# Issuing the first store of a streaming softmax without waiting for the third load

## The chip, the cores and the metric

The kernel runs on one core of a Trainium2 chip. The metric is the device time of one execution in microseconds. It was 317.92 us before the change, the median of 3 runs (317.4 to 318.28).

## The reference

```python
x = np.random.randn(32, 512, 1024).astype(np.float32)      # temperature = 0.5

def reference(x, temperature):
    scaled = x / temperature
    shifted = scaled - np.max(scaled, axis=-1, keepdims=True)
    exp_x = np.exp(shifted)
    return (exp_x / np.sum(exp_x, axis=-1, keepdims=True)).astype(np.float32)
```

It is a softmax over rows of 1024 numbers, 16384 rows, 67.1 MB in and 67.1 MB out.

## The kernel before

The 16384 rows are cut into eleven passes. A pass puts `k` rows side by side into each of the 128 partitions: 11 in the first pass, 12 in the nine after it, 9 in the last. A pass is one load into one tile `xt` (SP, L62), work in place, and one store of the same tile (L110). The stores of passes 0 to 5 are issued by Pool (`BY_POOL = 6`), the others by ACT. There are four tiles, `BUFS = 4`: four loads are issued at the start, and load i+4 goes out (from `store`) once store i has landed and its tile is free.

A pass is worked in groups of rows: 4, 4, 3 in the first, 6, 6 in the middle ones, 4, 3, 2 in the last (`PASSES`). For a group, `maximum` takes the row maxima on DVE (L71) and scales them to a bias (L74); `exponential` does one activation for each row on ACT, which also sums (L80); `divide` takes the reciprocal (L92) and multiplies on DVE, row by row (L98) or, in passes 2, 3, 4 and 6, the whole group at once (L95). The order is written out by hand (`tc.manual_schedule`): up to the last pass, the divide of a group comes after the maximum and the exponentials of the next group, and with the divide of a pass's last group comes its store. So the first store is due after the maximum of pass 1's first group and the divide of pass 0's third group.

The first store alone has an operation of Pool ahead of it: a copy of one column of `tiles[2]`, the tile of the third load, into a small tile `seen` that nothing reads (L108). The copy waits until the third load has landed; the store's issue is behind it in Pool's order.

Of the kernel before, what the change touches and what calls it, by code (L numbers as in the profile page):

```python
# [1 line left out]

# [4 lines left out]

PASSES = [[4, 4, 3]] + [[6, 6]] * 9 + [[4, 3, 2]]  # L10
BUFS = 4

WHOLE = (2, 3, 4, 6)


BY_POOL = 6

ALONE = 9

HELD = len(PASSES) - 1  # L20


@with_exitstack
def kernel(
    ctx: ExitStack,
    tc: tile.TileContext,
    x: bass.AP,
    temperature: bass.AP,
    out: bass.AP,
):  # L30
    nc = tc.nc
    f32 = mybir.dt.float32
    scale = 1.0 / float(temperature)
    extreme = mybir.AluOpType.max if scale > 0 else mybir.AluOpType.min

    P = 128
    xf = x.flatten_outer_dims()
    of = out.flatten_outer_dims()
    n, d = xf.shape
    rows = [sum(ks) for ks in PASSES]  # L40
    assert sum(rows) * P == n

    data = ctx.enter_context(tc.tile_pool(name="data", bufs=BUFS))
    stats = ctx.enter_context(tc.tile_pool(name="stats", bufs=4))


    groups = []
    for i, ks in enumerate(PASSES):
        for j, k in enumerate(ks):
            groups.append((i, sum(ks[:j]), k))  # L50

    def dram(t, i):
        block = t[P * sum(rows[:i]) : P * sum(rows[: i + 1]), :]
        return block.rearrange("(p k) d -> p k d", p=P, k=rows[i])

    tiles, small = [], []

    def load():
        i = len(tiles)
        if i < len(PASSES):  # L60
            xt = data.tile([P, rows[i], d], f32, name="xt")
            nc.sync.dma_start(out=xt, in_=dram(xf, i))  # L62
            tiles.append(xt)

    def maximum(g):
        i, a, k = groups[g]
        top, bias, sums, recip = (
            stats.tile([P, k], f32, name=name) for name in ("top", "bias", "sums", "recip")
        )
        small.append((bias, sums, recip))  # L70
        nc.vector.tensor_reduce(  # L71
            out=top, in_=tiles[i][:, a : a + k, :], axis=mybir.AxisListType.X, op=extreme
        )
        nc.vector.tensor_scalar_mul(bias, in0=top, scalar1=-scale)  # L74

    def exponential(g):
        i, a, k = groups[g]
        bias, sums, _ = small[g]
        for b in range(k):
            nc.scalar.activation(  # L80
                tiles[i][:, a + b, :],
                tiles[i][:, a + b, :],
                mybir.ActivationFunctionType.Exp,
                bias=bias[:, b : b + 1],
                scale=scale,
                accum_out=sums[:, b : b + 1],
            )

    def divide(g):
        i, a, k = groups[g]  # L90
        _, sums, recip = small[g]
        nc.vector.reciprocal(recip, sums)  # L92
        if i in WHOLE:
            xt = tiles[i][:, a : a + k, :]
            nc.vector.tensor_mul(xt, xt, recip.unsqueeze(2).to_broadcast([P, k, d]))  # L95
            return
        for b in range(k):
            nc.vector.tensor_scalar_mul(  # L98
                tiles[i][:, a + b, :], in0=tiles[i][:, a + b, :], scalar1=recip[:, b : b + 1]
            )  # L100

    def store(g):
        i, a, k = groups[g]
        if a + k == rows[i]:
            if i == 0:


                nc.gpsimd.tensor_copy(stats.tile([P, 1], f32, name="seen"), tiles[2][:, 0, 0:1])  # L108
            queue = nc.gpsimd if i < BY_POOL else nc.scalar
            queue.dma_start(out=dram(of, i), in_=tiles[i])  # L110
            load()

    with tc.manual_schedule():
        for _ in range(BUFS):
            load()
        waiting = []

        def finish():  # L120
            for g in waiting:
                divide(g)
                store(g)
            waiting.clear()

        for g, (i, a, k) in enumerate(groups):
            if i >= ALONE and a == 0:
                finish()
            maximum(g)
            exponential(g)  # L130
            if i < HELD:
                finish()
            waiting.append(g)
        finish()


# [1 line left out]
_INS = ['x', 'temperature']  # L138
_OUTS = [((32, 512, 1024), 'float32')]

_NUMBERS = {'temperature': 0.5}


# [26 lines left out]
```

## Time and profile before

| | us |
|---|---|
| median of 3 runs | 317.92 (317.4 to 318.28) |
| the profiled execution, its own time | 318.96 |
| its span in the profile | 317.2 |
| DVE busy | 252.3 (80%) |
| ACT busy | 148.3 (47%) |
| Pool busy | 3.7 (1%) |
| moved by DMA | 134.24 MB, 423 GB/s on the mean |

The span runs from the first to the last instruction of the program; the execution's own time also has what lies around it. The profile cuts the span into 40 slices of 7.93 us; a digit is a busy share in tenths. DVE is the vector engine, ACT the scalar engine, Pool the GpSimd engine, and SP the one that issues the loads. The 16 DMA engines of the core carry the packets of all queues; each load or store is split over all 16, and the trace holds start, duration, queue and size of every packet, and when each of the 16 parts of a transfer landed.

### The profile page before, as it was taken

The numbers are of one execution on the slowest core, as the hardware profiler recorded it, in microseconds if no ns is written. First come the engines' busy times: TensorE is split into PE (matmuls) and PEld (weight loads), VectorE is DVE, ScalarE is ACT, GpSimd is POOL, SyncE is SP. The second block draws the span as 40 slices with busy tenths as digits, with TensorE's granted clock in tenths as the row PEclk, the third lists the DMA queues.
The fourth block names the chain that finished last, engine by engine and source line by source line (L and its number), as shares of the span: only waits on it lengthen the run. The fifth ranks groups of instructions, "written<-read, shape, count | busy, mean of one in ns | idle before, by whom it ended". The sixth has DMA issues, their size and how long they took to land. (4 is left out here: it accounts for less than half of the span.)

```text
span 317.2 us, 542 instructions
## 1 busy us (share of the span) xinstructions
DVE 252.3 (80%) x160; ACT 148.3 (47%) x257; POOL 3.7 (1%) x11
## 2 busy tenths in 40 slices
DVE  0099999999999799969949994997199689779900
ACT  0048477468174353807171770438035805916600
POOL 0000010000000000000000000000000000000000
DMA  9999999999999999999999999999999999999994
GB/s 364 401 459 397 459 434 377 417 439 438 440 403 465 428 409 471 410 440 440 403 471 415 415 477 397 446 441 409 465 421 409 471 418 431 442 414 459 421 432 181
DMA packets 3171, 134.24 MB, mean 423 GB/s; under 512 B 352, under 2 KB 352, under 8 KB 352
## 3 DMA queue, kind: packets, MB, share of 16 engines
q1 hardware_dynamic: 1584, 67.11, 49.5%
q0 software_dynamic: 864, 37.22, 27.1%
q10 hardware_dynamic: 720, 29.88, 21.8%
q14 instruction: 3, 0.02, 0.0%
HBM read 67.11 MB, written 67.11 MB: 423 GB/s over the span
## 5 line engine op out<-in xcount | busy, mean ns | idle before, releaser
L80 ACT ACTIVATE xt<-xt,bias 128x1024 f32<-128x1024 f32 x128 | 145.2, 1135 | 133.7 <-DVE bias L74 64.6
L71 DVE TENSOR_REDUCE top<-xt 128x6 f32<-128x6144 f32 (+3 forms) x24 | 140.1, 5837 | 40.7 <-DMA xt<-in_x_dram 40.7
L98 DVE TENSOR_SCALAR xt<-xt,recip 128x1024 f32<-128x1024 f32 x80 | 54.5, 748 | 0.6
L95 DVE TENSOR_TENSOR xt<-xt,recip 128x6144 f32<-128x6144 f32 x8 | 52.5, 6559 | 0.6 <-DVE recip L92 0.2
L80 ACT ACTIVATION_READ_ACCUMULATOR xt<-xt,bias 128x1 f32 x128 | 23.8, 186 | 0.0
L80 ACT ACT_TABLE_LOAD x1 | 1.3, 1283 | 16.7 <-DMA xt<-in_x_dram 16.7
L92 DVE RECIPROCAL recip<-sums 128x6 f32<-128x6 f32 (+3 forms) x24 | 4.3, 180 | 5.8 <-ACT xt L80 5.8
L110 POOL DMA_DIRECT2D out_dram<-xt x6 | 3.3, 554 | 129.0 <-ACT xt L80 83.8
L74 DVE TENSOR_SCALAR bias<-top 128x6 f32<-128x6 f32 (+3 forms) x24 | 4.1, 171 | 0.8
L108 POOL COPY seen<-xt 128x1 f32<-128x1 f32 x1 | 0.2, 183 | 45.3 <-DMA xt<-in_x_dram 45.3
L151 POOL MEMSET const-bfloat16-1.0<- 128x1 bf16 x1 | 0.1, 102 | 0.0
L151 POOL MEMSET const-uint8-127<- 128x1 uint8 x1 | 0.1, 102 | 0.0
L151 POOL MEMSET const-float32-0.0<- 128x1 f32 x1 | 0.1, 99 | 0.2 <-issue 0.2
L151 POOL MEMSET const-float32-1.0<- 128x1 f32 x1 | 0.1, 99 | 0.0
## 6 DMA issues: line engine op xcount, KB each, us to landing
xt<-in_x_dram SPq DMA_DIRECT2D x9, 6144.0 KB, 37.1
out_dram<-xt POOLq DMA_DIRECT2D x5, 6144.0 KB, 36.7
out_dram<-xt ACTq DMA_DIRECT2D x4, 6144.0 KB, 32.6
xt<-in_x_dram SPq DMA_DIRECT2D x1, 5632.0 KB, 15.8
out_dram<-xt POOLq DMA_DIRECT2D x1, 5632.0 KB, 28.5
xt<-in_x_dram SPq DMA_DIRECT2D x1, 4608.0 KB, 39.5
out_dram<-xt ACTq DMA_DIRECT2D x1, 4608.0 KB, 15.5
```

The source lines that it names most:

```text
L71: nc.vector.tensor_reduce(out=top, in_=tiles[i][:, a : a + k, :], axis=mybir.AxisListType.X, op=extreme)
L74: nc.vector.tensor_scalar_mul(bias, in0=top, scalar1=-scale)
L80: nc.scalar.activation(tiles[i][:, a + b, :], tiles[i][:, a + b, :], mybir.ActivationFunctionType.Exp, bias=bias[:, b : b + 1], scale=scal ...
L92: nc.vector.reciprocal(recip, sums)
L95: nc.vector.tensor_mul(xt, xt, recip.unsqueeze(2).to_broadcast([P, k, d]))
L98: nc.vector.tensor_scalar_mul(tiles[i][:, a + b, :], in0=tiles[i][:, a + b, :], scalar1=recip[:, b : b + 1])
L108: nc.gpsimd.tensor_copy(stats.tile([P, 1], f32, name="seen"), tiles[2][:, 0, 0:1])
L110: queue.dma_start(out=dram(of, i), in_=tiles[i])
L151: nc = _bacc.Bacc("TRN2", target_bir_lowering=False, num_devices=1)
```

## The change

Pool's copy of the column of the third tile is taken out. Pool's first instruction after the start is now the issue of the first store, which waits for the divide of pass 0's last group. Nothing else in the order of any engine differs. The third store, also on Pool, now carries its own wait for the third load, which the copy had before.

```diff
     def store(g):
         i, a, k = groups[g]
         if a + k == rows[i]:
-            if i == 0:
-
-
-                nc.gpsimd.tensor_copy(stats.tile([P, 1], f32, name="seen"), tiles[2][:, 0, 0:1])
             queue = nc.gpsimd if i < BY_POOL else nc.scalar
             queue.dma_start(out=dram(of, i), in_=tiles[i])
             load()
```

## The prediction

> **What bounds the kernel now.** I read the strip of slices first, because a streaming kernel is bounded either by its transfers or by an engine that feeds them.
>
> ```profile
> DVE  0099999999999799969949994997199689779900
> ACT  0048477468174353807171770438035805916600
> ...
> DMA  9999999999999999999999999999999999999994
> GB/s 364 401 459 397 459 434 377 417 439 438 440 403 465 428 409 471 410 440 440 403 471 415 415 477 397 446 441 409 465 421 409 471 418 431 442 414 459 421 432 181
> ```
>
> The DMA row is at 9 in every slice but the last, so the transfers are the bound. The GB/s row scatters because a transfer's packet counts where it starts. Summed packet by packet over 10 us, the trace's packet records give 430 to 434 GB/s in every stretch from 10 us to 310 us, except 40 to 50 us (413) and 50 to 60 us (404). Those two stretches hold the only visible loss, and the edit lies in them. So I read that place in order of time next (columns: start, duration, engine and line, operation, idle time before it).
>
> ```profile
> 41.99 2.08 DVE L98 TENSOR_SCALAR xt<-xt,recip 128x1024 f32<-128x1024 f32 x3
> ...
> 43.98 6.54 DVE L71 TENSOR_REDUCE top<-xt 128x6 f32<-128x6144 f32 x1
> ...
> 45.70 0.18 POOL L108 COPY seen<-xt 128x1 f32<-128x1 f32 x1 [45.25 <-DMA xt<-in_x_dram]
> 46.28 0.67 POOL L110 DMA_DIRECT2D out_dram<-xt  x1 [0.40 <-issue]
> ...
> 66.09 0.53 POOL L110 DMA_DIRECT2D out_dram<-xt  x1 [19.15 <-DVE xt L98]
> ```
>
> The first tile is divided at 41.99 + 2.08 = 44.07. Pool copies at 45.70, when the third load has landed, and issues the first store at 46.28. The next store leaves 0.30 us after its divide (61.72 + 4.07 = 65.79, issued at 66.09). Then the waits (columns: total us, times, longest).
>
> ```profile
> POOL seen L108 <- DMA xt<-in_x_dram: 45.3, 1, 45.3
> ...
> DVE top L71 <- DMA xt<-in_x_dram: 40.7, 8, 16.6
> ```
>
> and SP's own:
>
> ```profile
> SPq L62 <- DMA out_dram<-xt: 238.8, 7, 72.2
> ```
>
> SP's line shows the ring that carries the kernel: SP holds load i+4 until store i has landed. DVE's line shows that DVE starves for loads, not the reverse. Last, the chain of waits at its end (start, duration, what):
>
> ```profile
> 208.96 35.04 DMA out_dram<-xt
> ...
> 244.14 39.52 DMA xt<-in_x_dram
> ...
> 283.68 4.43 DVE top L71
> ...
> 299.31 0.75 DVE xt L98
> ```
>
> A store lands, the last load is issued, lands at 283.66, and DVE and ACT finish by 300.7; the last store is issued at 300.76 and lands at 316.29.
>
> The whole time adds up from the transfers. A 48 KB packet of one DMA engine takes 1.812 us undisturbed (16 x 49152 B / 1.812 us = 434 GB/s). 134.22 MB / 434 GB/s = 309.3 us. Engines start at 1.95 us on the mean, the first packets take 0.74 us extra, and the disturbance near 50 us takes 1.13 us (the excess over 1.812 us of all packets that begin between 46 and 53 us is 18.0 us, over 16 engines). That is 313.1; the engines end their last packets at 312.9 to 313.9, with one at about 314.4 and the last one at 315.96. That one lag of some 2.6 us sets the end. The span is 317.2, the execution's own time 318.96, 1.0 above the median of 317.92 of the runs shown (317.4 to 318.28). I work in differences and put them on 317.92.
>
> **The change part by part.**
>
> *Removed: the copy on Pool.* 0.18 us of an engine that is busy 3.7 us in all, the wait for the third load, and 0.40 us between copy and issue. None is on the path by itself. Pool needs no new wait for the first store; the third store now itself waits for the third load, but it leaves at 93.12 and that load landed at 45.65: nothing.
>
> *Moved: the first store's issue.* 44.07 + 0.30 (row of the second store) = 44.37 in place of 46.28: 1.9 us earlier. One DMA moves, of 5632 KB; no other issue moves on Pool, and SP's four first loads are already queued (issued 0.74 to 2.1 us), so it passes nothing in a queue. What it moves past is the bytes of the fourth load.
>
> *When its bytes flow.* Its first packets began at 51.19, 4.9 us after the issue; with the same delay at 49.3. In the 4.9 us the engines were not idle: load packets ran until 48.3 at full rate. So the early store doesn't fill a hole; it swaps its bytes with bytes of the fourth load.
>
> *The fourth load.* From 51.2 on, load and store packets alternate. One store packet more ahead of its end (45056 B, 1.66 us) moves its landing from 71.29 to about 73.0. DVE first reads that tile at 79.13, so 6.1 us of cover remain; if that cover were gone, each us beyond it would be a us of DVE, which the later starvation by loads (40.7 us in all) would absorb again.
>
> *The store's landing, and the ring.* This is the decisive step. The store lands when the four loads and it are through: 2 x 5.767 + 3 x 6.291 = 30.41 MB / 434 GB/s = 70.1; + 1.95 + 0.74 + 1.13 = 73.9. Measured: 73.97 on the first engine, 74.80 on the last. As long as the fourth load is through before the store (71.3 before, 73.0 after), the order of the two has no effect on this instant. The fifth load is therefore issued at 74.87 as now, and from there on every transfer, wait and divide stands as before. Gain from the move itself: 0.
>
> A rule that speaks against the change: the Trainium skill, DMA: Bandwidth & Descriptors, section "Queues, rings and completion order", says that a DMA engine takes turns between the queues at packet granularity, so an early store takes every second packet from a load. The alternating packets agree. By the rule alone the fourth load would lose up to half of its rate for 1.9 us, about 1 us, also inside the cover.
>
> *The disturbance near 50 us.* In before, load packets that began at 48.3 to 50.6, 2 to 4 us after the issue, took 0.4 to 1.55 us longer than 1.812 us. None of the later stores shows this: around 66 to 72, 93 to 99 and 209 to 215 the rate is 424 GB/s or more. Whatever it is, it belongs to the first store, which the changed kernel has too, so I take 1.13 us again, about 1.9 us earlier. Its bounds: 0 (the later stores' rows), a gain of 1.1 us; and two slow packets on each engine in place of one at the worst row (2 x 1.55 = 3.1), a loss of 2.0 us. I take the nearest row, the same store's own: 0.
>
> A second rule bears here: the Trainium skill, SBUF — State Buffer, in its note on VectorE blocking DMA, says that descriptors of a Pool DMA cannot be written while VectorE runs an operation in a mode that uses both ports. In the trace VectorE runs one reduction from 43.98 to 50.52, over the old issue and the new one, and no other operation until 50.56; by the page's section on that contention a reduction doesn't block. By this rule the cost is 0 too; had the store been issued among the three divides it would have been up to 2.1 us.
>
> *The end.* The last load could come later only by the ring. The last store is issued at 300.76, its data could flow about 1.0 us later (the first load: 0.74 to 1.76), and the engine that ends last is free for it only at 305.07: 3.3 us of cover on that engine.
>
> Sum: 0 + 0 + 0 + 0 = 0, 317.9 us.
>
> **The rivals.**
>
> *Faster: the early start counts.* If the disturbance is the price of the store meeting a particular packet of the fourth load, or of the Pool work just ahead, it may go: 1.1 us, 316.8. If also the last engine's lag shrinks by part of its 2.6 us, 315.8. For it: the stretch 44 to 52 us is the only one that loses rate. Against it: loads ran at 434 GB/s until 48.3, so an earlier start by itself fills nothing.
>
> *Slower: the disturbance grows.* Place: the load packets in flight 2 to 4 us after the first store's issue. Now the third load's last packets and their completions (44.6 to 45.65) lie just there, and Pool's issue no longer comes after them. If each engine takes two slow packets instead of one, the cost is another 1.1 us at the mean and up to 2.0 us: 319.0 to 319.9. The trace already has a few engines with two slow packets in succession (1.0 + 0.4 us). It decides from a mean excess of 2.1 us on, or if the one late engine is hit by as much alone, since that engine sets the end. Against it: the third load is through at 45.65, before the expected new place (46.4).
>
> *The change does nothing to the order:* the copy could only be replaced by a wait of the same length if the divide were late; its end at 44.07 says it isn't. This rival gives 317.9 as well and differs only in the issue time.
>
> **How the numbers follow.** 0.3%, or 0.95 us, is about what a measurement of this kernel can tell from no change. No change, by the sum, including the last rival: 0.42, its own range 317.0 to 318.9. Slower by the disturbance or by the late engine: 0.34, since the excess of a single packet scatters from 0.4 to 1.55 us and the end hangs on one engine of sixteen, which can lose more easily than win. Faster: 0.24. Range 316.6 to 320.0: it takes in the price of a vanished disturbance (316.8) and of a doubled one at its worst (319.9); about 1 in 10 is left out on either side.
>
> **What would show it.** Right: Pool's first store issued at 44.3 to 44.5; the fourth load landing at about 73 and still before DVE's reduction at 79; the fifth load issued at 74.5 to 75.2; the same dip of rate, now around 46 to 51 us; the last store issued at 300 to 301.5. Wrong: the fifth load issued more than 1 us away from 74.87, a dip of rate that is absent or twice as deep, DVE waiting for the fourth tile, or one DMA engine that ends 4 us or more behind the others.

## The result and the profile after

The changed kernel is slower, by 0.7%: 320.69 us, the median of 22 runs (317.75 to 323.9), against 317.27 us for 22 runs of the kernel before (316.85 to 318.28). The ratio is 1.0072, 95% interval 1.005 to 1.0094; it leaves out the runs more than 1.5% above the fastest of the same kernel, and over all runs the medians stand 1.1% apart. The runs tell more than the median: the quickest (317.75) come near those of the kernel before, but 17 of 22 lie above 318.5 us, and none of the kernel before's 22. In later sittings the kernel before had such long executions too, 23 of 115, from 1 of 25 in one sitting to 9 of 31 in another, so every run below stands beside the kernel before of its own sitting. The profiled execution of the changed kernel is one of the short ones, 317.76 us with a span of 316.0 us. It cannot show the loss by itself; longer executions do, below.

The strip of the changed kernel:

```profile
DVE  0089999999999599969967994999299699689800
...
DMA  9899998999999999999999999999999999999995
GB/s 354 383 492 398 436 460 376 461 400 477 404 398 442 454 398 473 423 399 485 411 398 485 411 423 467 404 443 442 411 467 423 404 443 425 434 465 417 429 431 247
```

The transfers are still the bound. In order of time (start, duration, engine and line, operation, idle time before it), Pool's first instruction is now the store:

```profile
41.99 2.08 DVE L98 TENSOR_SCALAR xt<-xt,recip 128x1024 f32<-128x1024 f32 x3
...
43.99 6.55 DVE L71 TENSOR_REDUCE top<-xt 128x6 f32<-128x6144 f32 x1
...
44.38 0.67 POOL L106 DMA_DIRECT2D out_dram<-xt  x1 [43.94 <-DVE xt L98]
```

The waits (total us, times, longest) on loads and on landed stores have hardly moved:

```profile
DVE top L71 <- DMA xt<-in_x_dram: 39.4, 8, 16.6
```

```profile
SPq L62 <- DMA out_dram<-xt: 239.2, 7, 72.1
```

The end of the chain of waits in this short execution (start, duration, what):

```profile
210.05 34.35 DMA out_dram<-xt
...
244.53 37.57 DMA xt<-in_x_dram
...
282.12 4.43 DVE top L71
```

and in another execution of the same kernel that took 320.47 us (run again1):

```profile
209.66 34.91 DMA out_dram<-xt
...
244.70 40.48 DMA xt<-in_x_dram
...
285.21 4.43 DVE top L71
```

The last load is issued at the same time, but lands at 282.10 in one and at 285.19 in the other. A transfer has landed when the last of its 16 parts has. In the long execution the median part of that load landed at 277.36, the last but one at 280.10 and the last at 285.19: one DMA engine is 7.8 us behind the median. What that does to the rest shows in the windows near the end of the long execution (columns: window and length, busy time of DVE, ACT and Pool, clock, DMA share, GB/s):

```profile
300.00:302.00 2.00, 1.96 (x5) 0.21 (x2) 0.00 (x0) 1.00 0.91 393
302.00:304.00 2.00, 0.26 (x1) 0.00 (x0) 0.00 (x0) 1.00 0.70 301
304.00:308.00 4.00, 0.00 (x0) 0.00 (x0) 0.00 (x0) 1.00 1.04 445
```

At 302 to 304 us the DMA engines run dry: by the packet records 14 of 16 wait 0.4 to 1.1 us for the last store, which could only be issued at 302.29. Its last part landed at 317.82, in the short execution at 315.10. In the kernel before the same window reads

```profile
302.00:304.00 2.00, 0.00 (x0) 0.00 (x0) 0.00 (x0) 1.00 1.21 522
```

I call the landing of a transfer's last part minus that of its median part the lag. The table has it for the second store (landing near 100 us), the fifth (near 188 us) and the sixth (217 to 223 us), and then the landing of the end. "Excess" is the time by which load packets of 48 KB near the first store's start exceed 1.812 us: the sum over 16 engines divided by 16, and the largest single packet. All are single executions, us.

| run | first store issued | excess, mean / largest | lag, 2nd store | lag, 5th store | lag, 6th store | last part of last store | own time |
|---|---|---|---|---|---|---|---|
| before | 46.28 | 1.09 / 1.55 | 0.67 | 1.45 | 3.56 | 316.29 | 318.96 |
| delay | 45.99 | 1.23 / 1.49 | 0.54 | 0.53 | 0.93 | 314.78 | 317.45 |
| before_pool | 46.44 | 1.07 / 1.09 | 0.44 | 0.71 | 0.88 | 314.89 | 317.92 |
| delay12 | 48.44 | 1.15 / 1.30 | 0.38 | 0.59 | 0.83 | 314.47 | 317.13 |
| delay9 | 47.31 | 1.19 / 1.32 | 0.82 | 0.81 | 3.36 | 316.53 | 319.19 |
| delay3 | 45.08 | 1.17 / 1.27 | 0.81 | 1.26 | 3.97 | 316.96 | 319.63 |
| changed kernel | 44.38 | 0.41 / 0.89 | 1.95 | 1.95 | 1.96 | 315.10 | 317.76 |
| again2 | 44.63 | 0.70 / 1.30 | 2.09 | 2.07 | 4.09 | 316.40 | 319.06 |
| again1 | 44.66 | 1.04 / 1.50 | 0.94 | 2.07 | 4.61 | 317.82 | 320.47 |
| copy_tile1 | 44.24 | 0.74 / 1.06 | 0.61 | 2.58 | 5.92 | 318.03 | 320.70 |
| after_pool | 44.59 | 0.50 / 1.14 | 2.17 | 3.22 | 3.78 | 318.80 | 321.83 |

The time is the landing of the last part plus 2.7 us (3.0 where Pool issues the last store) in every row. The median engine differs less: its part of the last store landed at 313.65 in before, at 313.40 in the changed kernel and between 313.1 and 313.8 in the other rows but again1 (314.50) and copy_tile1 (314.72), where most engines stood idle for the last store. Time is lost on single engines.

### The profile page after: what moved, and what is told of

Same layout as the page of the kernel before. It is cut to its first block, busy times and chain, and to the rows that moved or that the text cites. A ratio compares the mean times of both kernels' runs of the same rounds, so it can differ in the third digit from the quotient of the medians.

```text
span 316.0 us, 539 instructions
## 1 busy us (share of the span) xinstructions
DVE 252.3 (80%) x160; ACT 148.3 (47%) x257; POOL 3.5 (1%) x10
```

## The experiments

**The changed kernel again (again1, again2).** No edit.

> The changed kernel once more, unaltered, to see an execution of the long kind (its runs lie between 317.8 and 323.9 us, the kernel before within 316.9 to 318.3). Theory A (the first store's earlier packets leave one DMA engine behind, and the run ends with that engine): a long execution ends with one engine 3 to 6 us behind the median one, the rate elsewhere 430 GB/s or more. Theory B (reads and writes of all engines disturb each other, by the relative position of load and store): every engine is late, and stretches well after 60 us run below 425 GB/s. Theory C (the last load lands late and leaves the DMA engines idle at the end): idle engines between 300 and 306 us.

> The changed kernel a third time, for another trace, with the same expectations as the second: one engine 3 to 6 us behind (theory A), all engines late with low rates after 60 us (theory B), or idle engines near the end (theory C).

again1: 320.86 us median of 6 runs (319.18 to 323.18). Its trace is the long execution above: theory A in its core, one engine far behind with the rest together, and the idle engines of theory C as its consequence. The rate over any 10 us from 60 to 300 us stays at 430 GB/s or more, so theory B falls for this run. again2 (319.06 us) ends with a lag of 2.86 us; three engines are behind together there, which is not the picture of theory A. In again2, and in the first trace of the changed kernel, load packets were longer a second time, at 76 to 96 us (0.49 and 0.53 us for each engine on the mean; before has 0.04 there), and over 10 us the rate fell to 419 and 411 GB/s. That is the mark of theory B, so theory B is out for again1 alone.

**The copy without its wait (copy_tile1).**

```diff
-                nc.gpsimd.tensor_copy(stats.tile([P, 1], f32, name="seen"), tiles[2][:, 0, 0:1])
+                nc.gpsimd.tensor_copy(stats.tile([P, 1], f32, name="seen"), tiles[1][:, 6, 0:1])
```

> The copy is kept, but it reads the tile of the second load, which landed at 31 us, so it waits for nothing new and the store leaves at about 44.9. If the wait for the third load, or the later issue, is what counts: median 320 to 321, spread over 6 us like the changed kernel. If Pool's copy ahead of its first DMA counts by itself: 317.3, spread of 1.4 us like the kernel before.

**A delay without that wait (delay).**

```diff
-                nc.gpsimd.tensor_copy(stats.tile([P, 1], f32, name="seen"), tiles[2][:, 0, 0:1])
+                seen = stats.tile([P, 128], f32, name="seen")
+                for _ in range(6):
+                    nc.gpsimd.tensor_copy(seen, tiles[0][:, rows[0] - 1, 0:128])
```

> In place of the one copy that waits for the third load, six copies of 128 columns of the first tile's last row, which wait only for its divide and for each other; by the row of the single copy (0.18 us and 0.40 us to the issue) 1.5 to 3 us of delay, issue at 46 to 47.5. If only the instant of the issue counts: 317.3 with a spread of 1.4 us. If Pool's wait on the landing of the third load counts in another way: 320 to 321 with the wide spread.

Pool's rows in order of time, first of copy_tile1, then of delay:

```profile
44.24 0.67 POOL L110 DMA_DIRECT2D out_dram<-xt  x1 [13.02 <-DVE xt L98]
```

```profile
43.99 2.06 POOL L110 COPY seen<-xt 128x128 f32<-128x128 f32 x6 [43.54 <-DVE xt L98]
45.99 0.66 POOL L112 DMA_DIRECT2D out_dram<-xt  x1
```

copy_tile1 keeps a copy and loses the wait: 320.22 us (10 runs, 316.98 to 321.36), ratio 1.0065 (1.003 to 1.0101). delay waits for no load and puts the issue at 45.99: 317.31 us (10 runs, 316.84 to 318.85) beside 317.32 of the kernel before, ratio 0.9982 (0.9955 to 1.0009). So neither the copy nor the wait for the third load counts. The instant of the issue does.

**A sweep of the instant (delay3, delay9, delay12, delay14, delay19).** The same edit with 3, 9, 12, 14 and 19 copies.

> Three copies of the first tile ahead of the first store instead of six: issue at about 45.0 us (six copies took 2.06 us from 43.99), between the changed kernel (44.4) and the kernel before (46.3). If the issue must come after the third load is through (45.65, a threshold): median 320 to 321. If every instant but a narrow one around 44.2 to 44.7 is good: 317.3. In both, a long run is one in which one of the 16 DMA engines lands its part of the last load 6 us or more behind the median engine, and a short one keeps it under 5 us.

> Nine copies: issue at about 47.0 us. By the threshold at the third load's landing: 317.3, narrow, like the kernel before. If the store's arrival counts by its place between two packets of a load (1.81 us each, bad at 44.2 to 44.7 and, as load and store alternate, again about 3.6 us later at 47.9 to 48.3): 317.3 too.

> Twelve copies: issue at about 48.0 us, one load packet and one more (3.6 us) after the changed kernel's. By the threshold: 317.3, narrow. By the place between two packets with that period: 319.5 to 321, wide again.

> Fourteen copies, issue of the first store at about 49.1 us. So far: median 320 to 321 at 44.2 to 44.7, 318.2 at 45.1, 317.3 at 46.0, 317.2 at 46.3, 319.0 at 47.3, 317.5 (in two groups, 317.1 and 319.4) at 48.4. If the number of load packets left on each engine when load and store begin to alternate counts (six in the changed kernel, five at 45.1 to 46.3, four at 47.3; even is bad, odd is good), three are left here: 317.2, narrow. If it is chance that the instant only shifts, a spread over 2 us or more, median 317.5 to 319.5.

> Nineteen copies, issue at about 50.9 us, two load packets left: by the even and odd rule 319 to 320.5, with no run below 317.2 in most; by chance, as the run with fourteen copies.

| issue (profiled run) | run | median | lowest to highest | runs above 318.5 | same for the kernel before beside it |
|---|---|---|---|---|---|
| 44.24 | copy_tile1 | 320.22 | 316.98 to 321.36 | 8 of 10 | 7 of 21 |
| 44.66 | again1 | 320.86 | 319.18 to 323.18 | 6 of 6 | 7 of 21 |
| 45.08 | delay3 | 318.17 | 317.23 to 320.11 | 4 of 10 | 2 of 25 |
| 45.99 | delay | 317.31 | 316.84 to 318.85 | 2 of 10 | 7 of 21 |
| 47.31 | delay9 | 318.98 | 317.19 to 320.15 | 7 of 10 | 2 of 25 |
| 48.44 | delay12 | 317.54 | 316.95 to 319.99 | 4 of 10 | 2 of 25 |
| 49.08 | delay14 | 318.68 | 317.27 to 320.01 | 6 of 10 | 1 of 25 |
| 51.16 | delay19 | 319.14 | 317.24 to 319.84 | 7 of 10 | 1 of 25 |

Every rule that I had laid down for the good and the bad instants fell. A threshold at the third load's landing (45.65) is refuted by delay9, which comes after it and takes 319.0. The period of two packets asked 317.3 of delay9 and a bad delay12. The rule of even and odd asked a narrow 317.2 of delay14. Only the reading by chance (a spread over 2 us, 317.5 to 319.5) fits delay14 and delay19. The mark that delay3's expectation set for a long execution, 6 us of lag at the last load, missed too: its 319.63 us had 5.28. What stands is that long executions occur at every instant, that their share depends on it, and that the instants of 46.0 and 46.3 us have the smallest. The loss at 44.2 to 44.7 is the largest of the sweep. At the later instants Pool also makes more copies ahead of the store; no run parts the two.

**The early store on SP's queue (sp_first).**

```diff
-            queue = nc.gpsimd if i < BY_POOL else nc.scalar
+            queue = nc.sync if i == 0 else nc.gpsimd if i < BY_POOL else nc.scalar
```

> The first store leaves as early as in the changed kernel, but on SP's queue, behind the fourth load in the same queue, so its packets don't alternate with that load's: the fourth load lands at about 59.5, the store still at 73.9 to 74.8 and the fifth load is issued at about 74.9. If the early alternation of load and store puts a DMA engine behind: 317.0 to 317.6, narrow. If the early store costs by itself, however it is queued: 320 to 321.

328.29 us (4 runs), and no answer to its question: with the store on SP the order of SP's waits changed, and the fifth load left at 89.54 instead of 74.9, after the second store's landing. Between 88 and 90 us the engines moved 64 GB/s. One thing is of use: load packets were again up to 1.2 us longer at 55.6 to 58.1 us, ahead of this store's first packets, though it came from SP's queue, and the rate at Pool's first store near 70 us did not dip.

**A known lag on one engine (one_engine, all_engines, one_small, one_half).** Into the kernel before, behind the four first loads (in all_engines the same bytes, split evenly over the 16 engines; in one_small and one_half a single row of 3067 and 6143 numbers; shown as one_engine has it, without the switch to the form of all_engines):

```diff
+        sink = nc.dram_tensor("sink", [2, 12281], f32, kind="Internal").ap()
+        for r in range(2):
+            flat = xf[12 * r : 12 * r + 12, :].rearrange("a b -> (a b)")
+            nc.sync.dma_start(out=sink[r : r + 1, :], in_=flat[0:12281].rearrange("(o n) -> o n", o=1))
```

> The kernel before, with two extra copies of 49 KB inside DRAM, queued on SP behind the four first loads, each of which one DMA engine alone carries (a single row of 12281 numbers). If the end is set by the DMA engine that is furthest behind (the lag), the run grows by up to the time of these two on that engine, 2 x 1.81 = 3.6 us by the rate of a 48 KB packet, less what that engine was ahead of the slowest (1 to 2.6 us in the traces): 318.2 to 321. If the total of bytes is what counts, 0.2 us at the most (98 KB at 434 GB/s): 317.4.

> The kernel before with the same two extra copies, but each split over all 16 DMA engines: 0.2 us more work on each. By both readings 317.2 to 317.6; it shows that the bytes and the issues themselves cost nothing much.

> The kernel before with one extra copy of 12 KB inside DRAM on one DMA engine (a row of 3067 numbers, queued behind the first loads): 0.45 us of that engine at the rate of a 48 KB packet. If a lag of one engine is carried to the end as it is: at most 0.5 us more, 317.3 to 317.7, narrow. If a small early lag of one engine is made larger on the way: more than twice that, 318.2 to 320, with a spread like the changed kernel's.

> The same with 24 KB, 0.9 us of one engine. Carried as it is: 317.3 to 318.2. Made larger: 319 to 321.

98 KB on one engine cost 4.1 us: 321.35 (4 runs) beside 317.26, ratio 1.0117 (1.0098 to 1.0135). The same bytes over all engines cost 0.6 us: 317.83 (10 runs, 317.6 to 318.37), ratio 1.0018 (1.0008 to 1.0027). Both lie 0.2 to 0.4 us above what I expected at the most. The chain of one_engine shows the last load issued at 246.99, 2.9 us later than in before, and the strip a hole of the DMA near 300 us, where the others wait:

```profile
DMA  8999999989999999999999999999999999999793
```

```profile
211.88 34.97 DMA out_dram<-xt
...
246.99 39.76 DMA xt<-in_x_dram
```

So the lag of one engine sets the time, at its full price: 4.1 less the 0.6 of the two transfers as such is 3.5 us, for two packets of 1.81 us. one_small (0.45 us of one engine) took 317.85 with 3 of 10 runs above 319.5, one_half (0.9 us) 318.69 with 5 of 10 above 319. Added to the 317.31 of the kernel before beside them these are 0.5 and 1.4 us, between my two expectations, and 9 of 31 runs of that kernel were above 318.5 there too. Neither ratio is clear of no change (0.9953 to 1.0032, 0.9996 to 1.0071). Whether a small lag is carried or made larger on the way, these two don't settle.

**All stores by Pool (before_pool, after_pool).** `BY_POOL = 11` in both kernels.

> The kernel before with all eleven stores issued by Pool, so that no second store queue begins at 209 us. The reference for the next run; by itself 316.9 to 318.5, since Pool is idle, unless the issue by Pool delays the last store.

> The changed kernel with all eleven stores issued by Pool. If the change of store queues at 209 us (where in long executions the landing of the sixth store falls from 218.5 to 221 to 223 us) is what makes an engine's lag larger: no more than 0.5 us above the run with Pool stores and the copy, spread under 2 us. If the lag grows in other places: 2 to 3.5 us above it, spread of 4 us or more.

before_pool took 317.80 (10 runs, 317.42 to 318.31), after_pool 319.22 (10 runs, 317.1 to 322.33). A wide spread and a loss of 1.4 us stay without the second store queue, between my two expectations (0.5 us at the most, or 2 to 3.5), so the change of queues at 209 us isn't the whole cause.

The traces say that it has a part. With ACT taking over, the medians of copy_tile1 and again1 stood 2.9 and 3.5 us above the kernel before beside them (2.1 and 3.2 us by the ratios); next to 1.4 that alone decides little. But the lag jumps at the sixth store, the one in flight when ACT takes over. In 7 of the 18 traces with two store queues the lag of the sixth store is at most 0.4 us above that of the fifth, and these executions took 317.1 to 318.3 us. In the other 11, before among them (1.45, then 3.56), it is 1.9 to 5.0 us above it, and they took 318.96 us or more. With all stores on Pool it rose by 0.2 and 0.6. before_pool had no run of 10 above 318.5 us, the kernel before beside it 9 of 31, which are few runs to go by. So in the traces the executions of 319 us and more go with a jump at that change of queues, after_pool excepted. What decides whether the lag jumps there is not shown.

In the trace of after_pool the lag is 0.40 at the fourth load, 0.86 at the first store, 2.17 at the second, and then 3.22, 4.71 and 5.68 at the fifth, seventh and last. At the first store's start one engine had two load packets that were 1.14 and 0.60 us too long, while the mean over all engines was 0.50. The trace doesn't name a packet's engine, so it is not shown that this is the one that lags.

**A row ahead (early_row_after, early_row_before).** In each kernel Pool stores row 0 of the first pass once the first group is divided; the first store has the other ten rows.

```diff
+        if g == 0:
+            nc.gpsimd.dma_start(out=dram(of, 0)[:, 0:1, :], in_=tiles[0][:, 0:1, :])
 ...
-            queue.dma_start(out=dram(of, i), in_=tiles[i])
+            if i == 0:
+                queue.dma_start(out=dram(of, i)[:, 1:, :], in_=tiles[i][:, 1:, :])
+            else:
+                queue.dma_start(out=dram(of, i), in_=tiles[i])
```

> The changed kernel, but the first row of each partition's first pass is stored by Pool on its own as soon as the first group is divided (29 us), 0.5 MB; the other ten rows follow at 44.4 as in the changed kernel. If the disturbance comes with the first store of the program (in the run on SP's queue it came with that store, at 56 to 61 us, and not with Pool's first), it moves to 31 to 36 us, the ten rows start at 49 us without it, and the 16 engines stay together: part landings of the second store within 1 us, 317.0 to 318.0, narrow. If an early store is bad by its instant alone: 319 to 321, spread 4 us.

> The same early row in the kernel before, with the copy: the reference of the last run. 317.0 to 318.0 by either reading, with the dip of rate at 31 to 36 us by the first.

Both expectations missed. The row left at 27.3 and no load packet before 46 us was lengthened; the disturbance stayed with the bulk of the store (46.4 to 53.8 and 48.0 to 50.1 us). early_row_before took 318.19 (10 runs, 317.32 to 319.5), early_row_after 326.63 (4 runs, 322.41 to 329.38). In the trace of early_row_after fifteen engines send their first packet of the ten rows at 50.2 to 50.8 and one at 48.7; one engine is out of step from there, and the lag is 5.75 us at the second pass's store and 13.0 us at the sixth's. So the instant of the bulk decides, with a row ahead of it too.

**What follows.** In four of six traces with the bulk issued at 44.2 to 44.7 us (changed kernel, again2, after_pool, early_row_after) one to three engines were 1.95 us or more behind the median at the second pass's store. In early_row_after one engine was out of step from the first store's first packets. In the changed kernel and again2 the second stretch of long load packets, at 76 to 96 us, lies before that store too. In none of the traces with the issue at 45 us or later was that lag over 0.83 us, apart from one_engine, where it was put in. In the other two, again1 and copy_tile1, the lag near 100 us was 0.94 and 0.61 and grew after it, to 4.61 and 5.92 at the sixth store; as far as packets can be followed, with load packets of that engine that took 0.2 to 1.0 us longer, and with the jump at the change of queues.

## Why the prediction was wrong

The steps that concern all engines together held. The issue was put at 44.37 and came at 44.38. The fourth load was to land at about 73.0 and landed at 72.38 (73.35 in again1), before DVE's reduction at 79.06. The store was to land, and the fifth load to be issued, at 74.87 as before: 74.77, and 74.44 to 75.09 in again1, again2 and copy_tile1. So up to the fifth load the forecast of no gain from the move was right within 0.5 us. The store's first packets came at 48.62, not at 49.3: 4.2 us after the issue instead of 4.9.

On the fourth load, the turn-taking rule of the Trainium skill (DMA: Bandwidth & Descriptors, "Queues, rings and completion order") gave an estimate of about 1 us later; the trace has 72.38 - 71.29 = 1.09. again2 has 1.28 and again1 2.06, so my own term, one whole store packet of 1.66 us, lies within what the runs show, and the estimate by the rule at its lower end. Neither bears on the end, since DVE reads that tile later in all of them.

The step that failed is "The store's landing, and the ring", where it says that from the fifth load on "every transfer, wait and divide stands as before". It treats the 16 engines as one. The prediction had seen that one engine's lag "sets the end", and then counted the disturbance by its mean. The mean near the first store in fact fell, from 1.09 to between 0.41 and 1.04, and stays at 1.2 or less with the second stretch at 76 to 96 us. So the slower rival "the disturbance grows", which asked for 2.1 or more, is refuted in its main form. The faster rival had a disturbance that shrank, and no gain from it: the fastest of 22 runs took 317.75. What changed is how the cost falls on the engines: lags of 1.95 to 2.17 us at the second store in the changed kernel, again2 and after_pool, where before had 0.67. The rival's second condition, "if the one late engine is hit by as much alone", names the right place.

The step "The end" failed with it. It set 3.3 us of cover against a late last load and did not ask whether the same engine's lag, which delays that load, would also grow: the last load's landing lag was 4.4 us in before, and 7.8 and 8.5 in again1 and copy_tile1. The slower price, 319.0 to 319.9, was made from packets near 50 us alone and left out what is added in the following 250 us, above all the jump of the lag at the sixth store, 2.5 us in again1 and 3.3 in copy_tile1. The profile that the sum was read from had that jump as well: it is a long execution of the kernel before (318.96 us), and the lag of 2.6 us at its end, which the sum takes as fixed, is 0.7 to 1.2 us in delay12, delay and before_pool. The range ended at 320.0, the median was 320.69.

The second rule, on descriptors that VectorE keeps Pool from writing, was not put to a clean test. One run issued the store beside divides, delay19 (Pool, then VectorE):

```profile
51.16 0.90 POOL L112 DMA_DIRECT2D out_dram<-xt  x1
...
51.19 4.07 DVE L98 TENSOR_SCALAR xt<-xt,recip 128x1024 f32<-128x1024 f32 x6
```

The issue took 0.90 us, where the other large first stores on Pool took 0.53 to 0.67, and its first packets came 5.7 us after it, within the 4.0 to 6.3 us of those stores with the issue at 44.2 to 49.1. That neither shows a block nor excludes one.

The rival that the change does nothing to the order is out, since the issue did move.

Open is why the instant decides which engines fall behind and how far, and why a lag grows in one execution and not in the next, at the change of store queues and elsewhere. The long load packets of a lagging engine are the place where time is lost in the traces; what makes them long is not shown. No version tried was faster than the kernel before by more than its interval.

## What to carry to other kernels

Where DMA is the bound, read the landing of each transfer's 16 parts, not its end alone: the time was the landing of the last part plus a constant, while the median engine's part moved by 0.7 us between nine of eleven traces. A small edit that leaves every engine's bytes alone can still cost about 1% through single DMA engines that fall behind, so compare some twenty runs and their spread, not one profile. A wait that looks useless may only be a delay that happens to sit at a good instant; test it by replacing it with a delay that waits for nothing. Where another engine takes over the issue in mid-kernel, read the lag on both sides of it.

## What the runs showed of the hardware

- One DMA engine with 98 KB more cost 4.1 us; the same bytes over 16 engines cost 0.6 us.
- When the first large store began beside running loads, 48 KB load packets took up to 1.55 us longer than their 1.812 us. In two of the traces with the early store there was a second stretch of it at 76 to 96 us (up to 0.97 us). A 0.5 MB store with 4 KB packets ahead of the large one neither showed this (0.1 us at the most) nor took it away.
- That 0.5 MB store needed 19.9 us (27.33 to 47.18 us) beside loads with 48 KB packets. Each engine had 8 of its packets, one every 1.97 us with a load packet of 1.81 us between two: the two queues took turns by packets, not by bytes.
- The engines alternate a load packet and a store packet. An engine that fell behind at the start stayed behind to the end in after_pool (lag 2.17 us at the second store, 5.68 at the last) and early_row_after (5.75 and 3.31).
- Where the issue of the stores passes from Pool to ACT at 209 us, the lag grew by 1.9 us or more from the fifth to the sixth store in 11 of 18 traces; where all stores are Pool's, by 0.2 and 0.6.
